# A scan's exponentials moved into the block of short products, in a one-core hybrid encoder layer

## The chip, the core and the metric

The kernel runs on one core of one Trainium2 chip. The metric is the device time of one execution in microseconds, the median of the runs shown. The engines are named as in the profile: PE (matrix products; PEld is its weight load), DVE, ACT, POOL, and SP, which here only issues DMAs.

## What is computed

One layer of a streaming encoder for 256 frames of a new stream and 8 x 16 frames of running streams, 384 tokens in all, model width 2048. Float32 accuracy is kept by splitting each operand into a high and a low part and taking three products.

```python
proj = u @ p['w_in']                      # pool | z | x, B, C | dt | gates
xbc, new_conv = causal_conv(xbc, st_conv, p['conv_w'], p['conv_b'])
...
def step(h, inp):                         # the scan, per chunk
    cum = jnp.cumsum(dtc * A, axis=1)
    seg = cum[:, :, None] - cum[:, None, :]
    decay = jnp.exp(jnp.where(causal, seg, -jnp.inf))
    cb = jnp.einsum('btgn,bsgn->btsg', Cc, Bc)
    y = jnp.einsum('btsgr,bsgrp->btgrp', cb[..., None] * decay, xdt)
    y = y + jnp.einsum('btgn,bgrpn->btgrp', Cc, h) * jnp.exp(cum)[..., None]
    h = h * jnp.exp(last)[..., None, None] + jnp.einsum('bsgn,bsgr,bsgrp->bgrpn', Bc, w_end, xdt)
...
h = y * silu(z)                           # gated RMSNorm, one norm per group
m = sigmoid(g_A) * (A @ w_pool_proj) + sigmoid(g_B) * (B @ w_ssd_proj);  x += RMSNorm(m @ w_out)
x += RMSNorm(relu(RMSNorm(x) @ w_up)^2 @ w_down)
```

The scan has 8 groups of 8 heads. The change lies in this scan, which takes the stretch from 478 to 1300 us of the span.

## The kernel before

The scan phase walks over the 8 groups. Per group there are ten projections of 128 channels by 384 tokens: B, C, x0 to x3 and z0 to z3. Each is two *units* (`proj_units`), one for each half of the 2048 input channels: a weight tile of 128 x 1024 is loaded, split (`wh` by a copy on ACT, `wl` by a subtraction on DVE; `wturn`), and multiplied by 24 matmuls (`half`, L188 to L190). `flow` sets the order on all engines, as the code is recorded in one order and each engine works through its part in that order. For unit i it issues the load of unit i + 4 on SP, the products of unit i on PE, the split of unit i + 3 (`prep`), then the unit's eviction `post`, and then `work`, which takes tasks from the queue `todo` until their costs have used up the budget of a unit. `need` empties that queue up to a named task. The pools hold three tiles of weights, three of each split part (every fourth pair has buffers of its own, L143 and L144), and PSUM has two banks for projections (`banks(mm=2, ss=6)`), so that a projection has to wait until the one before the last is evicted.

A *block* (`block(old, new)`) is a run of short products on PE: `Y` of the older half group (masked decay times values, L677), `yi` of the newer one (state times C, L697), the older one's new prompt state `pp`, and transposes of the newer one's x (and of B, with `cb`, at a first half). DVE then evicts: `yis`, the older x with its skip, `xdt` and `xdw` (x by dt and by the decay to the end), `cbm`. Each group has two blocks: that of its first half stands behind x2's second unit, that of its second half behind z3's.

After a block, tasks go into `todo`:

- `state_tasks`: the part of `xdw` for the running streams is split (`xhl`: ACT, then DVE, L797 and L798) and written by SP to `x_scr`. `xst_load` reads it back in another layout (L907), behind eight loads `bst_load` (L898) at a first half. `update` multiplies it by B (`su`, L920, PE) and adds it to the state `hs` (L924, DVE). The update of a first half stands between the two units of z1, that of a second half between the two units of the next group's x0.
- `decay_state`: the state is multiplied by its decay (L782).
- `decay_tasks`: per pair of heads a tile `E` of exponentials from `cbc` (cumulative sums, broadcast by a load on SP): 8 short calls and two longer ones on ACT.
- `gated_tasks`: `zs` times `xs` on DVE, the square (`ssum`, `ysq`) on ACT.
- `decay_masks`: `E` times `cbm` on DVE (L861).

ACT holds one table of functions at a time; the order has an ACT_TABLE_LOAD wherever exponentials follow `silu` or the reverse.

Of the kernel before, what the change touches and what calls it, by code (L numbers as in the profile page):

```python
# [7 lines left out]
F32 = mybir.dt.float32  # L8
F32R = mybir.dt.float32r
I32 = mybir.dt.int32  # L10
AF = mybir.ActivationFunctionType
ALU = mybir.AluOpType
# [3 lines left out]
P = 128  # L16
T = 384
TP = 256
NB = 8
# [3 lines left out]
G = 8  # L23
# [39 lines left out]
def build(ctx, tc, io):  # L63
    nc = tc.nc
    v, s, te, gp, sy = nc.vector, nc.scalar, nc.tensor, nc.gpsimd, nc.sync
# [48 lines left out]
    def later(cost, tag, f):  # L114
        todo.append((cost, tag, f))
# [9 lines left out]
    def need(*tags):  # L125
        while any(t in tags for _, t, _ in todo):
            cost, _, f = todo.popleft()
            f()
            debt[0] -= cost
# [123 lines left out]
    x_scr = [dram.tile([P, 2, 2, P], F32, name=f"x_scr{i}") for i in range(16)]  # L253
# [117 lines left out]
    decb = small.tile([P, NH, NB], F32, name="decb")  # L371
    with tc.tile_pool(name="phc", bufs=1, reuse_waits="tile") as pc, tc.tile_pool(name="phc2", bufs=2, reuse_waits="tile") as pc2:
        bufs = []
        for i in range(2):
            b = pc.tile([P, 519], F32, name=f"pbuf{i}")
# [173 lines left out]
    nothing = lambda *_: None  # L549
    phd = ExitStack()  # L550
    pd = phd.enter_context(tc.tile_pool(name="phd", bufs=2, reuse_waits="tile"))
# [8 lines left out]
    for i in range(2):  # L560
        b = pd1.tile([P, 24, 19], F32, name=f"cbuf{i}")
# [87 lines left out]
        sy.dma_start(hs, io["ssm"][g * 2 + hf])  # L649

    def cbc_load(g, hf):
        need(f"exp{g}_1" if hf else f"exp{g - 1}_3")
        for j in (hf * 2, hf * 2 + 1):
            cbc = S[g]["cbc"][j] = pd.tile([P, 2, T], F32, tag="cbc", name=f"cbc{g}_{j}")
            sy.dma_start(cbc, cum_scr[g * 8 + j * 2 : g * 8 + j * 2 + 2, :].partition_broadcast(P))
# [10 lines left out]
    def block(old, new):  # L666
        Y = []
        if old:
            g, hf = old
            need(f"E{g}_{hf * 2}", f"E{g}_{hf * 2 + 1}")  # L670
            d = S[g]
# [13 lines left out]
        if new:  # L685
            g2, h2 = new
# [5 lines left out]
            hs = d2["hs"][h2]  # L692
# [70 lines left out]
                cbm = d2["cbm"] = pd.tile([P, 512], F32, tag="cbm", name=f"cbm{g2}", bufs=1)  # L763
                v.tensor_tensor(cbm, cb, cst2[:, :512], ALU.mult)
        if new:
            state_tasks(g2, h2)
            decay_state(g2, h2)
            decay_tasks(g2, h2)
            final = new == (G - 1, 1)
            if final:  # L770
                decay_masks(g2, h2)
        if old:
            gated_tasks(g, hf)
        if new and not final:
            decay_masks(g2, h2)

    def decay_state(g, hf):
        hs, h0 = S[g]["hs"][hf], g * 8 + hf * 4

        def decay():  # L780
            hv = hs.rearrange("p b (h q) -> p b h q", h=4)
            v.tensor_tensor(  # L782
                hv,
                hv,
                decb[:, h0 : h0 + 4, :].rearrange("p h b -> p b h").unsqueeze(3).to_broadcast([P, NB, 4, 64]),
                ALU.mult,
            )

        later(2.3, f"dec{g}_{hf}", decay)

    def state_tasks(g, hf):
        d = S[g]

        def parts():
            xhl = pd.tile([P, 2, 2, P], F32R, tag="xhl", name=f"xhl{g}_{hf}", bufs=1)
            x = d["xdw"][hf][:, :, 2, :]
            s.activation(xhl[:, 0], x, AF.Copy)  # L797
            v.tensor_tensor(xhl[:, 1], x, xhl[:, 0].bitcast(F32), ALU.subtract)  # L798
            sy.dma_start(x_scr[g * 2 + hf], xhl.bitcast(F32))

        later(0.5, f"xhl{g}_{hf}", parts)

    def gated_tasks(g, hf):
        d = S[g]

        def gated(j):
            z = d["zs"][j]
            v.tensor_tensor(z, z, d["xs"][j], ALU.mult)
            if j == 0:
                d["ssum"] = pd.tile([P, T], F32, tag="ssum", name=f"ssum{g}", bufs=1)  # L810
                s.activation(d["ssum"], z, AF.Square)
            else:
                d["q"] = pd.tile([P, T], F32, tag="ysq", name=f"ysq{g}_{j}", bufs=1)
                s.activation(d["q"], z, AF.Square)

        def add():
            v.tensor_tensor(d["ssum"], d["ssum"], d["q"], ALU.add)

        def parts():
            add()  # L820
            d["sh"] = pd.tile([P, T], F32R, tag="sh", name=f"sh{g}", bufs=1)
            d["sl"] = pd.tile([P, T], F32R, tag="sl", name=f"sl{g}", bufs=1)
            s.activation(d["sh"], d["ssum"], AF.Copy)
            v.tensor_tensor(d["sl"], d["ssum"], d["sh"].bitcast(F32), ALU.subtract)

        j = hf * 2
        later(0.6, f"gt{g}_{j}", lambda: (add() if j else None, gated(j)))
        later(0.6 if hf else 1.2, f"gt{g}_{j + 1}", lambda: (add() if j else None, gated(j + 1)))
        if hf:
            later(1.1, f"sum{g}", parts)  # L830

    def decay_tasks(g, hf):
        d = S[g]
        for j in (hf * 2, hf * 2 + 1):
            h0 = g * 8 + j * 2

            def head(hh, j=j, h0=h0):
                if hh == 0:
                    d["E"][j] = pd.tile([P, 2, 512], F32, tag="E", name=f"E{g}_{j}")
                E, cbc, h = d["E"][j], d["cbc"][j], h0 + hh  # L840
                s.activation(E[:, hh, P:TP], cbc[:, hh, P:TP], AF.Exp, bias=tok[:, 9, h : h + 1])
                for b, e0 in enumerate((0, TP, T)):
                    s.activation(
                        E[:, hh, e0 : e0 + P], cbc[:, hh, b * P : b * P + P], AF.Relu, bias=tok[:, b, h : h + 1], scale=-1.0
                    )

            def powers(j=j):
                E = d["E"][j]
                s.activation(E[:, :, :P], E[:, :, :P], AF.Exp, scale=-1.0)
                s.activation(E[:, :, TP:], E[:, :, TP:], AF.Exp, scale=-1.0)  # L850

            later(0.6, None, lambda head=head: head(0))
            later(0.8, f"exp{g}_{j}", lambda head=head, powers=powers: (head(1), powers()))

    def decay_masks(g, hf):
        d = S[g]
        for j in (hf * 2, hf * 2 + 1):

            def masked(j=j):
                E = d["E"][j]  # L860
                v.tensor_tensor(E, E, d["cbm"].unsqueeze(1).to_broadcast([P, 2, 512]), ALU.mult)  # L861

            later(1.3, f"E{g}_{j}", masked)
# [46 lines left out]
            )  # L910

    def update(g, hf):
        need(f"dec{g}_{hf}")
        hs, xst, bs = S[g]["hs"][hf], S[g]["xst"], bst
        su = []
        for r in range(4):
            o = sstile(f"su{g}_{hf}_{r}")
            su.append(o)
            for b in range(2):
                te.matmul(o[:, b * 256 : b * 256 + 256], bs[:, r, b, :], xst[:, r, :], start=True, stop=True)  # L920

        def add(r):
            hr = hs[:, r * 2 : r * 2 + 2, :].rearrange("p b n -> p (b n)")
            v.tensor_tensor(hr, hr, su[r], ALU.add)  # L924
            if r == 3:
                gp.dma_start(io["new_ssm_s"][g * 2 + hf], hs)

        for r in range(3, -1, -1):
            todo.appendleft((0.7, f"su{g}_{hf}" if r == 3 else None, lambda r=r: add(r)))
# [12 lines left out]
    for g in range(G):  # L942
        u0 = 17 + g * 10
        xu = lambda j: conv_units(u0 + 2 + j, g * 4 + j, "xs", 6, put(g, "xs", j))
        items += conv_units(u0, 32 + g, "BT", 1, put(g, "BT"))
        if g:
            at(xst_load, g - 1, 1)
        items += conv_units(u0 + 1, 40 + g, "CT", 1, put(g, "CT"), lambda g=g: make_Cm(g))
        u = xu(0)
        items += u[:1]  # L950
        if g:
            at(update, g - 1, 1)
        items += u[1:]
        at(cbc_load, g, 0)
        items += xu(1)
        u = xu(2)
        items += u[:1]
        items.append((*u[1][:3], nothing))
        at(block, (g - 1, 1) if g else None, (g, 0))
        at(u[1][3])  # L960
        u = xu(3)
        items += u[:1]
        at(lambda g=g: (need(f"su{g - 1}_1"), hs_load(g, 1)))
        items += u[1:]
        at(bst_load, g)
        at(xst_load, g, 0)
        items += z_units(g, 0)
        u = z_units(g, 1)
        items += u[:1]
        at(update, g, 0)  # L970
        items += u[1:]
        u = z_units(g, 2)
        items += u[:1]
        if g:
            at(norm_mm, g - 1)
        items += u[1:]
        u = z_units(g, 3)
        items += u[:1]
        at(cbc_load, g, 1)
        items += u[1:]  # L980
        at(block, (g, 0), (g, 1))
        if g < G - 1:
            at(lambda g=g: (need(f"su{g}_0"), hs_load(g + 1, 0)))

# [35 lines left out]
    at(update, G - 1, 1)  # L1020
    items += tail_[4:5]
    at(block, (G - 1, 1), None)
    at(narrow)
    items += tail_[5:8]
    at(norm_mm, G - 1)
# [201 lines left out]

    hs_load(0, 0)
    wide[0] = pd1
    begin, rest = flow(items, budget=3.2)  # L1230
    begin()
    xs2, pga_hold = [], ExitStack()

# [617 lines left out]
```

## Time and profile before

| what | us |
|---|---|
| median of 3 runs | 2798.18 (2797.39 to 2800.08) |
| profiled execution, its time | 2798.07 |
| its span | 2796.3 |
| PE busy | 2762.0 |
| DVE busy | 1825.3 |
| ACT busy | 1346.2 |
| scan phase (478 to 1300 us): PE, DVE, ACT busy | 799.15, 581.52, 453.08 of 822.0 |

A row of the timeline gives start and duration in us, the engine, the line of the kernel, the operation with the tile written and those read (buffer numbers left out), the shapes, how often it runs in a row, and in brackets how long the engine stood idle before it and what released it. A row of the waits gives the total in us, the times, and the longest. "SPq" is SP's queue of DMA issues. A DMA's start there is its issue, not its landing.

### The profile page before, as it was taken

The numbers are of one execution on the slowest core, as the hardware profiler recorded it, in microseconds if no ns is written. First come the engines' busy times: TensorE is split into PE (matmuls) and PEld (weight loads), VectorE is DVE, ScalarE is ACT, GpSimd is POOL, SyncE is SP. The second block draws the span as 40 slices with busy tenths as digits, with TensorE's granted clock in tenths as the row PEclk, the third lists the DMA queues.
The fourth block names the chain that finished last, engine by engine and source line by source line (L and its number), as shares of the span: only waits on it lengthen the run. The fifth ranks groups of instructions, "written<-read, shape, count | busy, mean of one in ns | idle before, by whom it ended". The sixth has DMA issues, their size and how long they took to land.

```text
span 2796.3 us, 38572 instructions
## 1 busy us (share of the span) xinstructions
PE 2762.0 (99%) x14961; PEld 2517.0 (90%) x14961; DVE 1825.3 (65%) x2421; ACT 1346.2 (48%) x2181; POOL 222.1 (8%) x334
## 2 busy tenths in 40 slices
PE   9999999999999999999999999999999999999998
PEld 9998888999999999998888888899999999998987
DVE  8755333667777767767533333648887788778878
ACT  6433323556556465564522223535555555555663
POOL 0000000000000000001000000000011111111221
PEclk9999999999999999999999999999999999999999
DMA  6444444456556555545844454444566868777787
GB/s 223 135 131 144 145 145 166 164 175 211 185 187 205 203 177 197 203 162 192 285 150 150 151 196 136 147 155 181 183 172 167 203 174 216 182 192 181 174 242 243
DMA packets 166328, 505.37 MB, mean 181 GB/s; under 512 B 20544, under 2 KB 39808, under 8 KB 161280
## 3 DMA queue, kind: packets, MB, share of 16 engines
q1 hardware_dynamic: 132000, 409.22, 42.9%
q0 software_dynamic: 34000, 93.68, 14.2%
q8 instruction: 117, 1.92, 0.3%
q14 instruction: 67, 0.55, 0.1%
q10 hardware_dynamic: 144, 0.01, 0.0%
HBM read 413.93 MB, written 88.90 MB: 180 GB/s over the span
## 4 chain that ended last, share of the span: by engine, by line
PE 80%; DVE 10%; ACT 5%; issue 2%; DMA 1%; SPq 0%; POOL 0%; DVEq 0%; ACTq 0%
PE pj_up L188 6%; PE pj_up L189 6%; PE pj_up L190 6%; PE wd L1507 5%; PE wd L1508 5%; PE wd L1506 5%; PE pj_sp L207 3%; PE pj_sp L209 3%; PE pj_sp L208 3%; PE pj_x L188 3%; PE pj_x L189 3%; PE pj_x L190 3%; PE pj_gb L207 2%; PE wo L208 2%; PE pj_ga L208 2%
## 5 line engine op out<-in xcount | busy, mean ns | idle before, releaser
L1360 ACT ACTIVATE wh_wd<-raw 128x1024 fp32r<-128x1024 f32 x210 | 222.8, 1061 | 255.3 <-PE pj_up L189 103.9
L188 PE MATMUL pj_up<-x1h,wh_up 128*128 128x384 f32 x992 | 334.1, 337 | 0.0
L189 PE MATMUL pj_up<-x1l,wh_up 128*128 128x384 f32 x992 | 333.3, 336 | 0.0
L190 PE MATMUL pj_up<-x1h,wl_up 128*128 128x384 f32 x992 | 333.3, 336 | 0.0
L1361 DVE TENSOR_TENSOR wl_wd<-raw,wh_wd 128x1024 fp32r<-128x1024 f32 x210 | 256.8, 1223 | 97.2 <-ACT wh_wd L1360 96.4
L188 PE MATMUL pj_x<-xgh,wh_x 128*128 128x384 f32 x768 | 257.8, 336 | 0.0
L190 PE MATMUL pj_x<-xgh,wl_x 128*128 128x384 f32 x768 | 256.7, 334 | 0.0
L189 PE MATMUL pj_x<-xgl,wh_x 128*128 128x384 f32 x768 | 256.6, 334 | 0.0
L1507 PE MATMUL wd<-wl_wd,fh 128*128 128x512 f32 x588 | 229.1, 390 | 0.2 <-DVE wl_wd L1361 0.2
L1506 PE MATMUL wd<-wh_wd,fh 128*128 128x512 f32 x588 | 229.0, 389 | 0.0
L1508 PE MATMUL wd<-wh_wd,fl 128*128 128x512 f32 x588 | 228.8, 389 | 0.0
L1360 ACT ACTIVATE wh_up<-w_up 128x1024 fp32r<-128x1024 f32 x123 | 130.2, 1059 | 127.7 <-issue 66.5
L188 PEld LDWEIGHTS pj_up<-x1h,wh_up 128*128 128x128 f32 x992 | 186.5, 188 | 4.0
L189 PEld LDWEIGHTS pj_up<-x1l,wh_up 128*128 128x128 f32 x992 | 186.5, 188 | 4.0
L190 PEld LDWEIGHTS pj_up<-x1h,wl_up 128*128 128x128 f32 x992 | 186.5, 188 | 0.0
L1361 DVE TENSOR_TENSOR wl_up<-w_up,wh_up 128x1024 fp32r<-128x1024 f32 x123 | 150.2, 1222 | 55.3 <-ACT wh_up L1360 55.3
L188 PE MATMUL pj_z<-xgh,wh_z 128*128 128x384 f32 x512 | 172.3, 337 | 11.0 <-DVE zs L641 11.0
L190 PE MATMUL pj_z<-xgh,wl_z 128*128 128x384 f32 x512 | 172.7, 337 | 9.0 <-DVE wl_z L104 9.0
L104 DVE TENSOR_TENSOR wl_sp<-w_sp,wh_sp 128x1024 fp32r<-128x1024 f32 x64 | 78.1, 1225 | 153.0 <-ACT wh_sp L103 152.6
L189 PE MATMUL pj_z<-xgl,wh_z 128*128 128x384 f32 x512 | 171.8, 336 | 0.0
L1522 POOL DMA_DIRECT2D acc_scr<-ev x144 | 122.9, 902 | 572.3 <-ACT ev L1518 567.5
L103 ACT ACTIVATE wh_sp<-w_sp 128x1024 fp32r<-128x1024 f32 x64 | 67.8, 1062 | 173.0 <-PE pj_sp L209 168.5
(373 smaller groups left out, 6626.1 us busy)
## 6 DMA issues: line engine op xcount, KB each, us to landing
w_up<-w_up SPq DMA_DIRECT2D x126, 512.0 KB, 5.2
raw<-w_down SPq DMA_DIRECT2D x112, 512.0 KB, 5.9
w_x<-w_in SPq DMA_DIRECT2D x96, 512.0 KB, 4.3
acc_scr<-ev POOLq DMA_DIRECT2D x168, 256.0 KB, 5.7
w_z<-w_in SPq DMA_DIRECT2D x64, 512.0 KB, 4.4
w_sp<-w_ssd SPq DMA_DIRECT2D x64, 512.0 KB, 3.3
w_ga<-w_gate SPq DMA_DIRECT2D x32, 512.0 KB, 3.3
w_pp<-w_pp SPq DMA_DIRECT2D x32, 512.0 KB, 3.2
```

What stands on the lines that cost most here:

```text
L188: te.matmul(out, wh, xh, start=first, stop=False)
L189: te.matmul(out, wh, xl, start=False, stop=False)
L190: return te.matmul(out, wl, xh, start=False, stop=last)
L207: te.matmul(o, ah, wh[:, c], start=k == 0, stop=False)
L208: te.matmul(o, ah, wl[:, c], start=False, stop=False)
L209: te.matmul(o, al, wh[:, c], start=False, stop=k == 2 * n - 1)
L1360: s.activation(h, w, AF.Copy)
L1361: return (h, l), lambda: v.tensor_tensor(l, w, h.bitcast(F32), ALU.subtract)
L1506: te.matmul(o, ah, wh[:, cols], start=c_first[c] == r and k2 == 0, stop=False)
L1507: te.matmul(o, ah, wl[:, cols], start=False, stop=False)
L1508: te.matmul(o, al, wh[:, cols], start=False, stop=c_last[c] == r and k2 == 1)
L1522: gp.dma_start(acc_scr[p][c], e, accum_op=ALU.add)
```

## The change

Five edits, all in the scan phase:

1. `decay_tasks` and the ACT part of `state_tasks` become `exponentials`, which the block calls at its end: both tiles of `E` are computed without a break, the copy of `xhl` between them. The low part of `xhl` and the write of `x_scr` stay a task.
2. The new function `behind` runs after the block and after the eviction of the projection: the state decay and the first of a half's two gated products are done there at once, no longer as tasks.
3. z3's eviction is moved behind the block of the second half, as x2's was at the first.
4. `cbc_load` and `update` no longer empty the queue up to the exponentials and the decay.
5. The scan's budget of a unit falls from 3.2 to 2.6.

```diff
     def cbc_load(g, hf):
-        need(f"exp{g}_1" if hf else f"exp{g - 1}_3")
...
         if new:
-            state_tasks(g2, h2)
-            decay_state(g2, h2)
-            decay_tasks(g2, h2)
-            final = new == (G - 1, 1)
-            if final:
-                decay_masks(g2, h2)
+            exponentials(g2, h2)
+
+    def behind(old, new):
+        if new:
+            decay_state(*new)
         if old:
-            gated_tasks(g, hf)
-        if new and not final:
-            decay_masks(g2, h2)
+            gated_tasks(*old)
+        if new:
+            decay_masks(*new)
...
     def gated_tasks(g, hf):
...
-        later(0.6, f"gt{g}_{j}", lambda: (add() if j else None, gated(j)))
+        if j:
+            add()
+        gated(j)
         later(0.6 if hf else 1.2, f"gt{g}_{j + 1}", lambda: (add() if j else None, gated(j + 1)))
...
-    def decay_tasks(g, hf):
+    def exponentials(g, hf):
         d = S[g]
+        x = d["xdw"][hf][:, :, 2, :]
         for j in (hf * 2, hf * 2 + 1):
             h0 = g * 8 + j * 2
...
+            E = d["E"][j] = pd.tile([P, 2, 512], F32, tag="E", name=f"E{g}_{j}")
+            cbc = d["cbc"][j]
+            for hh in range(2):
+                h = h0 + hh
                 s.activation(E[:, hh, P:TP], cbc[:, hh, P:TP], AF.Exp, bias=tok[:, 9, h : h + 1])
...
+            s.activation(E[:, :, :P], E[:, :, :P], AF.Exp, scale=-1.0)
+            s.activation(E[:, :, TP:], E[:, :, TP:], AF.Exp, scale=-1.0)
+            if j % 2 == 0:
+                xhl = pd.tile([P, 2, 2, P], F32R, tag="xhl", name=f"xhl{g}_{hf}", bufs=1)
+                s.activation(xhl[:, 0], x, AF.Copy)
+
+        def low():
+            v.tensor_tensor(xhl[:, 1], x, xhl[:, 0].bitcast(F32), ALU.subtract)
+            sy.dma_start(x_scr[g * 2 + hf], xhl.bitcast(F32))
+
+        later(0.5, f"xhl{g}_{hf}", low)
...
     def update(g, hf):
-        need(f"dec{g}_{hf}")
...
         at(cbc_load, g, 1)
-        items += u[1:]
+        items.append((*u[1][:3], nothing))
         at(block, (g, 0), (g, 1))
+        at(u[1][3])
+        at(behind, (g, 0), (g, 1))
...
-    begin, rest = flow(items, budget=3.2)
+    begin, rest = flow(items)
```

How this moves instructions is shown for group 1; the other groups are alike. In the names, `E1_0` is the tile of the group's first pair of heads, `wh_z1_0_1` the high part of the weights of z0's second unit (`z1_0` is z0 of group 1), `x6` is x2 of group 1, `x42` its successor's C.

On ACT, behind the block of group 1's first half, before the change:

```order
L760 ACTIVATE Bhl1_5400<-trB1_5375 128x128
L586 COPY cbuf0_3981<-cstate_3979 128x8x3
L588 COPY cbuf0_3981<-cbuf0_3981 128x15x3
L591 ACTIVATE cacc6_5409<-cbuf0_3981,vec_70 128x384
L592 COPY cstate_3979<-cbuf0_3981 128x27
L103 ACTIVATE wh_z1_0_1_5439<-w_z1_0_1_5299 128x1024
L600 ACTIVATE xs6_5446<-cacc6_5409,vec_70 128x384
L797 ACTIVATE xhl1_0_5448<-xdw1_0_5391 128x256
```

On ACT at the same place after it, the start and (behind the six other rows of `E1_1`) the end of the piece:

```order
L759 ACTIVATE Bhl1_5400<-trB1_5375 128x128
L825 ACT_TABLE_LOAD
L825 ACTIVATE E1_0_5406<-cbc1_0_5189,tok_689 128x128
L827 ACTIVATE E1_0_5406<-cbc1_0_5189,tok_689 128x128 x3
L825 ACTIVATE E1_0_5406<-cbc1_0_5189,tok_689 128x128
L827 ACTIVATE E1_0_5406<-cbc1_0_5189,tok_689 128x128 x3
L830 ACTIVATE E1_0_5406<-E1_0_5406 128x2x128
L831 ACTIVATE E1_0_5406<-E1_0_5406 128x2x256
L834 ACTIVATE xhl1_0_5417<-xdw1_0_5391 128x256
L825 ACTIVATE E1_1_5419<-cbc1_1_5191,tok_689 128x128
```

And its end:

```order
L831 ACTIVATE E1_1_5419<-E1_1_5419 128x2x256
L586 COPY cbuf0_3981<-cstate_3979 128x8x3
L588 COPY cbuf0_3981<-cbuf0_3981 128x15x3
L591 ACTIVATE cacc6_5433<-cbuf0_3981,vec_70 128x384
L592 COPY cstate_3979<-cbuf0_3981 128x27
L796 ACTIVATE ysq0_2_5439<-zs0_2_4783 128x384
L103 ACTIVATE wh_z1_0_1_5468<-w_z1_0_1_5299 128x1024
L600 ACT_TABLE_LOAD
```

A table load, two tiles of exponentials and a square now stand ahead of the conv's copy and of `wh_z1_0_1`; before, they followed seven to ten rows later.

On DVE, at the same block, behind the eviction of x2 (`cbuf0`), before the change:

```order
L587 TENSOR_TENSOR cbuf0_3981<-pj_x6_5270,rstd_159 128x24x16
L104 TENSOR_TENSOR wl_z1_0_1_5440<-w_z1_0_1_5299,wh_z1_0_1_5439 128x1024
L596 SCALAR_TENSOR_TENSOR cacc6_5409<-cbuf0_3981,vec_70,cacc6_5409 128x384 x3
L798 TENSOR_TENSOR xhl1_0_5448<-xdw1_0_5391,xhl1_0_5448 128x256
L782 TENSOR_TENSOR hs1_0_4915<-hs1_0_4915,decb_690 128x2048
L104 TENSOR_TENSOR wl_z1_1_0_5482<-w_z1_1_0_5412,wh_z1_1_0_5481 128x1024
```

On DVE after it:

```order
L587 TENSOR_TENSOR cbuf0_3981<-pj_x6_5270,rstd_159 128x24x16
L778 TENSOR_TENSOR hs1_0_4943<-hs1_0_4943,decb_690 128x2048
L799 TENSOR_TENSOR ssum0_4941<-ssum0_4941,ysq0_1_4979 128x384
L790 TENSOR_TENSOR zs0_2_4783<-zs0_2_4783,xs2_4515 128x384
L104 TENSOR_TENSOR wl_z1_0_1_5469<-w_z1_0_1_5299,wh_z1_0_1_5468 128x1024
L596 SCALAR_TENSOR_TENSOR cacc6_5433<-cbuf0_3981,vec_70,cacc6_5433 128x384 x3
L837 TENSOR_TENSOR xhl1_0_5417<-xdw1_0_5391,xhl1_0_5417 128x256
```

The decay and the gated product moved ahead of the split; the low part of `xhl`, which SP's write of `x_scr` waits for, still stands behind that split and the conv taps. SP's rows stand in the same order before and after.

On ACT, behind the block of group 1's second half, after the change (the row ahead of it is the second tile of exponentials; before, `wh_x42_1` stood directly behind the block's copy `pe`, ahead of the first exponential):

```order
L831 ACTIVATE E1_3_5919<-E1_3_5919 128x2x256
L642 ACT_TABLE_LOAD
L642 ACTIVATE zs1_3_5930<-zs1_3_5930 128x384
L793 ACTIVATE ssum1_5935<-zs1_0_5607 128x384
L143 ACTIVATE wh_x42_1_5966<-w_x42_1_5809 128x1024
```

There the weights of the next group's C wait for both tiles, a table load, z3's `silu` and a square.

More of the change, by code (lines that the diff above doesn't have):

```diff
@@ L765, in block @@
         if new:
-            state_tasks(g2, h2)
-            decay_state(g2, h2)
-            decay_tasks(g2, h2)
-            final = new == (G - 1, 1)
-            if final:
-                decay_masks(g2, h2)
+            exponentials(g2, h2)
+    def behind(old, new):
+        if new:
+            decay_state(*new)
         if old:
-            gated_tasks(g, hf)
-        if new and not final:
-            decay_masks(g2, h2)
+            gated_tasks(*old)
+        if new:
+            decay_masks(*new)
     def decay_state(g, hf):
         hs, h0 = S[g]["hs"][hf], g * 8 + hf * 4
[L780 to L801, printed above, removed]
+        hv = hs.rearrange("p b (h q) -> p b h q", h=4)
+        v.tensor_tensor(
+            hv,
+            hv,
+            decb[:, h0 : h0 + 4, :].rearrange("p h b -> p b h").unsqueeze(3).to_broadcast([P, NB, 4, 64]),
+            ALU.mult,
+        )
     def gated_tasks(g, hf):
@@ L830, in gated_tasks @@
             later(1.1, f"sum{g}", parts)
-    def decay_tasks(g, hf):
+    def exponentials(g, hf):
         d = S[g]
+        x = d["xdw"][hf][:, :, 2, :]
         for j in (hf * 2, hf * 2 + 1):
             h0 = g * 8 + j * 2
[L837 to L840, printed above, removed]
+            E = d["E"][j] = pd.tile([P, 2, 512], F32, tag="E", name=f"E{g}_{j}")
+            cbc = d["cbc"][j]
+            for hh in range(2):
+                h = h0 + hh
                 s.activation(E[:, hh, P:TP], cbc[:, hh, P:TP], AF.Exp, bias=tok[:, 9, h : h + 1])
@@ L845, in head @@
                     )
[L847 to L853, printed above, removed]
+            s.activation(E[:, :, :P], E[:, :, :P], AF.Exp, scale=-1.0)
[7 more added lines that the diff above has]
+        later(0.5, f"xhl{g}_{hf}", low)
     def decay_masks(g, hf):
@@ L960, in build @@
         at(u[1][3])
+        at(behind, (g - 1, 1) if g else None, (g, 0))
         u = xu(3)
@@ L1022, in build @@
     at(block, (G - 1, 1), None)
+    at(behind, (G - 1, 1), None)
     at(narrow)
```

## The prediction

> **What bounds the kernel now.** I read the page's busy times first, then the list of waits on PE, then one group of the scan instruction by instruction: PE, then ACT, DVE and SP's DMA queue around the same block. From the page:
>
> ```profile
> PE 2762.0 (99%) x14961; PEld 2517.0 (90%) x14961; DVE 1825.3 (65%) x2421; ACT 1346.2 (48%) x2181; POOL 222.1 (8%) x334
> ```
>
> PE is busy 99% of the span, so less work on ACT or DVE is worth nothing by itself. The change can only take away or add time in which PE stands still. The list of waits on PE (us in total, times, longest) has three rows over 1.2 us that lie in the scan:
>
> ```profile
> PE pj_z L188 <- DVE zs L641: 11.0, 8, 1.8
> PE pj_z L190 <- DVE wl_z L104: 9.0, 6, 1.5
> PE su L920 <- DMA xst<-x_scr: 1.5, 2, 0.9
> ```
>
> The first two are the prize: 20.0 us, about 2.5 in each of eight groups. The third is short, but it tells that the state update `su` starts as soon as its transfer has landed, in two groups out of eight even later than PE would like. PE around group 1's first half (start, duration):
>
> ```profile
> 592.58 1.11 PE L920 MATMUL su<-xst,bst 128*128 128x256 f32 x8
> 614.43 1.96 PE L677 MATMUL Y<-E,xdt 128*64 128x256 f32 x24
> ...
> 641.77 1.19 PE L920 MATMUL su<-xst,bst 128*128 128x256 f32 x8
> 648.50 0.41 PE L188 MATMUL pj_z<-xgh,wh_z 128*128 128x384 f32 x1 [1.37 <-DVE zs L641]
> ```
>
> Five half products lie between 593.5 (`su` 592.58 and its 0.95 us of issue) and 614.43, so a half product is 4.18 us: the pace at which split weights must arrive. ACT in the same stretch:
>
> ```profile
> 620.26 0.28 ACT L760 ACTIVATE Bhl<-trB 128x128 fp32r<-128x128 f32 x1
> ...
> 622.74 0.24 ACT L588 COPY cbuf<-cbuf 128x45 f32<-128x45 f32 x1 [2.10 <-DVE cbuf L587]
> ...
> 623.64 1.06 ACT L103 ACTIVATE wh_z<-w_z 128x1024 fp32r<-128x1024 f32 x1
> ...
> 628.36 0.40 ACT L797 ACTIVATE xhl<-xdw 128x256 fp32r<-128x256 f32 x1
> ...
> 636.57 1.28 ACT L841 ACT_TABLE_LOAD   x1
> ...
> 642.00 0.39 ACT L841 ACTIVATE E<-cbc,tok 128x128 f32<-128x128 f32 x1
> ...
> 645.17 0.51 ACT L814 ACTIVATE ysq<-zs 128x384 f32<-128x384 f32 x1
> 645.59 1.04 ACT L103 ACTIVATE wh_z<-w_z 128x1024 fp32r<-128x1024 f32 x1
> ```
>
> One tile of exponentials takes 3.17 us (642.00 to 645.17). The pair runs from 636.57 to 645.17, and the weights of z2 come behind it at 645.59: that is why PE stands at 648.50. DVE:
>
> ```profile
> 624.74 1.23 DVE L104 TENSOR_TENSOR wl_z<-w_z,wh_z 128x1024 fp32r<-128x1024 f32 x1 [2.03 <-ACT wh_z L103]
> 625.88 1.92 DVE L596 SCALAR_TENSOR_TENSOR cacc<-cbuf,vec,cacc 128x384 f32<-128x384 f32 x3
> 628.79 0.43 DVE L798 TENSOR_TENSOR xhl<-xdw,xhl 128x256 fp32r<-128x256 f32 x1 [0.99 <-ACT xhl L797]
> ...
> 651.57 2.35 DVE L861 TENSOR_TENSOR E<-E,cbm 128x1024 f32<-128x1024 f32 x2
> 653.84 2.35 DVE L104 TENSOR_TENSOR wl_z<-w_z,wh_z 128x1024 fp32r<-128x1024 f32 x2
> ```
>
> The second stall of a group (`pj_z L190`) waits for the split at 653.84, which the two masks at 651.57 hold up. And SP's queue, group 1 and the last group:
>
> ```profile
> 629.25 0.33 SPq L799 DMA_DIRECT2D x_scr<-xhl  x1
> ...
> 630.64 6.71 SPq L898 DMA_DIRECT2D bst<-b_scr  x8
> 637.40 1.85 SPq L907 DMA_DIRECT2D xst<-x_scr  x4
> 639.29 2.42 SPq L96 DMA_DIRECT2D w_z<-w_in  x3
> ```
>
> ```profile
> 1241.76 1.85 SPq L907 DMA_DIRECT2D xst<-x_scr  x4
> 1246.32 1.11 PE L920 MATMUL su<-xst,bst 128*128 128x256 f32 x8
> ```
>
> This is the row to remember. SP works in order: the write of `xhl` at 629.25, then a state load, a weight load, eight loads of `bst`, four of `xst`, the last issued by 639.25. `su` begins 2.5 us later, at 641.77. From the issue of that write to `su` it is 12.5 us with nothing to spare.
>
> **The change, part by part.** *Exponentials into the block.* In the first half of a group ACT now does, straight behind `Bhl` (free at 620.43): table load 1.28, two tiles 6.34 with the `xhl` copy 0.40 between them, the four small conv steps 1.0 (622.74 to 623.64, and 0.1), the square `ysq` 0.42, and only then the `wh_z` of z0's second half: it starts at 629.87 instead of 623.64 and ends at 630.93. PE needs it at 633.2 (three half products behind the block's end at 620.6), its low part at 633.5: DVE delivers that by 632.1. No stall there.
>
> *The low part of xhl.* Behind that split DVE does three conv taps (1.92), then `xhl` (0.43): 630.97 + 1.14 + 1.92 + 0.43 = 634.46, against 629.22 before. SP's write of `x_scr` leaves at 634.4 instead of 629.25, 5.1 us later (4.7 in group 0, which has no older block and so no `ysq`). Everything that SP has behind it moves along: state load, weight load, `bst`, `xst`. So `su` moves from 641.77 to about 646.9. On PE's path only the `su` of the first half counts: 7 x 5.1 + 4.7 = 40.4. Groups with some slack take less: the last group's `su` starts 2.71 behind its last issue, 0.2 more than group 1's 2.52. I take 0.15 a group, 1.2 in all: **+39 us**. Bounds: 0 if SP's stretch shrinks by as much (rival 1), 45 if each `su` moves by 5.6.
>
> *State decay and first gated product directly behind.* DVE does the 2.29 us decay, a sum and a product while it would wait for ACT anyway (from 622.65 to 630.9). Cost nothing; cover gone, 3.2 us, but ACT's 6 us are longer.
>
> *Eviction behind.* x2's was behind its block already. z3's product is evicted behind the four `xdw`, a few us later, and its PSUM bank is wanted two half products behind the block: hidden. x3's eviction follows the split of z1's first half, which is itself behind `xhl` and the next square, at about 638.3 by the same durations; PE's z1 begins about 1 us late; but PE then stands at `su` until 646.9 anyway, so this is inside the 39.
>
> *The stalls that go.* The exponentials are done by 628.5 and the masks run while PE waits at `su`; both stalls behind them go: **-20.0 us**. What is late next is the weight fetch of z2: it stands behind `xst` in SP's queue. Rows of SP's weight loads in the window from 639 to 641, us from issue to landing:
>
> ```profile
> DMA to landing us min/median/max: 4.6/4.9/5.3
> ```
>
> Issue + 4.9 + 1.04 (`wh`) + 1.14 (`wl`) + 0.55 (z0's eviction, which frees the bank) is 7.7 behind the last `xst`; PE comes there 2.5 + 0.95 + 4.18 = 7.6 behind it. I put 0.2 a group: **+2 us** (bounds 0 and 4).
>
> *The second half* has the same pile-up with more room. Rows of block (1,1) and the tail:
>
> ```profile
> 667.45 1.96 PE L677 MATMUL Y<-E,xdt 128*64 128x256 f32 x24
> 672.64 0.35 ACT L741 COPY pe<-pp 128x256 f32<-128x256 f32 x1
> 693.29 1.11 PE L920 MATMUL su<-xst,bst 128*128 128x256 f32 x8
> ...
> 1272.37 1.96 PE L677 MATMUL Y<-E,xdt 128*64 128x256 f32 x24
> ...
> 1295.12 1.12 PE L920 MATMUL su<-xst,bst 128*128 128x256 f32 x8
> ```
>
> ACT from at latest 672.9: load 1.28, tiles and copy 6.74, load back 1.28, `silu` and square 0.95, `wh` 1.06: 684.2; `wl` by 685.4. `pe` waited there for z3's eviction, which now comes later, so it can start some 0.6 earlier: 683.6 and 684.8. PE wants these at 684.9 and 685.3. `x_scr` then leaves at 685.2 to 685.9 (before: 677.4), and 2.2 + 2.5 + 2.5 later `su` could start: 693.1 at worst, needed at 693.29. So nothing is paid, barely. In the tail the units are shorter: the chain wants about 24.1 behind `Y` (17.7 + 2.2 + 1.8 + 2.5), PE is there after 22.75: **+1.3**.
>
> *Tables.* 13 of 52 loads go, 13 x 1.28 = 16.7 us of ACT, off PE's path; the one load that moves ahead of `wh_z` is in the sum above with 1.28. The Trainium skill ("ScalarE: Activation LUTs", What ACT_TABLE_LOAD costs) puts a switch at 2.66 us with its drain; by that the sum would be some 11 us worse. The trace disagrees: the load at 636.57 is followed by work in 1.3 us, so the row decides.
>
> *Sum*: 39 - 20.0 + 2 + 1.3 = +22.3 us. The profiled execution took 2798.07 us, within 0.1 of the median 2798.18; predicted 2820 us, 0.8% slower.
>
> **The rivals.** *1, faster: SP's stretch shrinks.* The eight `bst` issues take 6.71 us, and part of that is waiting for transfers:
>
> ```profile
> SPq L898 <- DMA w_z<-w_in: 10.1, 8, 1.4
> SPq L898 <- DMA hs<-ssm: 9.8, 8, 1.5
> ```
>
> That is 2.5 us a group. If that wait, and a similar part of the slow issues, were for loads already in flight before `x_scr`, they would be over by 634.4, and `su` would move by about 1.6 only: 8 x 1.6 - 20 + 1 = -6, **2792**. The sign turns at a shift of about 2.4 a group; at that point nothing is measured (2798). Against it: the state load and the weight load stand behind `x_scr` in the queue, so they move along.
>
> *2, the clock.* PE would stand about 4 us at each `su`, longer than anywhere now. A cold start is at the head of the trace, the first two products of one size:
>
> ```profile
> 4.70 0.65 PE L320 MATMUL pj_p<-xgh,wh_o 128*128 128x384 f32 x1
> 5.19 0.34 PE L321 MATMUL pj_p<-xgh,wl_o 128*128 128x384 f32 x1
> ```
>
> The cold one takes twice as long. If the clock fell at each wait and PE ran one half product at half speed before it is back, that costs up to 8 x 1.7 = 14: **2834**. The longest idle on PE in the scan now is under 2 us, and no drop is seen behind it. The Trainium skill ("TensorE: Matmul & The Clock Gate", Why this matters for your kernels) says to avoid gaps over about 3 us for this reason; no run here has shown such a gap yet.
>
> *3, the second half misses.* If its split comes 1 to 1.5 us late in seven groups, +9: **2829**. For it: a margin of 0.1 to 0.5 us, worked out over eight instructions.
>
> **How the numbers follow.** A difference under 0.2% (5.6 us) can't be told from none here. The forecast, 2820, has 0.60, with 2810 to 2829 as its own range; rival 1 0.07 for faster and 0.06 for a shift that just cancels; the clock 0.11; the second half 0.16. Slower is 0.60 + 0.11 + 0.16 = 0.87. The range runs from 2804, which leaves out the cases without a loss, to 2836, which takes in the clock's whole price.
>
> **What would show it.** In the changed kernel: `x_scr<-xhl` leaves some 14 us behind the block of a first half instead of 8.7; PE's list of waits has `su <- xst` with 30 to 40 us over eight waits of 3 to 5 us each, and the rows `pj_z <- zs` and `pj_z <- wl_z` shrink to a few us. The prediction is wrong if `su` starts as early as now behind its block, if PE waits at `pj_x` behind second halves, or if the granted clock dips at `su`.

## The result and the profile after

The changed kernel took 2838.3 us (median of four runs, 2835.4 to 2842.0), the kernel before 2798.6 (2797.4 to 2800.1) on the same chip: a ratio of 1.0142, interval 1.0125 to 1.0160. So it is 39.7 us slower, where 22 were predicted and 2836 was the upper end. The profiled execution took 2841.95 us (span 2840.2), the slowest of the four; against the span before, 2796.3, that is 43.9.

The page's busy times and the list of waits on PE, changed kernel (us in total, times, longest):

```profile
PE 2780.7 (98%) x14961; PEld 2530.3 (89%) x14961; DVE 1828.0 (64%) x2421; ACT 1333.5 (47%) x2168; POOL 221.5 (8%) x334
```

```profile
PE su L906 <- DMA xst<-x_scr: 30.5, 8, 5.7
PE pj_z L188 <- DVE cbuf L587: 9.6, 7, 1.4
PE su L906 <- DMA w_z<-w_in: 4.3, 1, 4.3
PE pj_x L190 <- DVE wl_x L144: 3.0, 5, 0.6
```

The two stalls that were to go (`pj_z <- zs`, `pj_z <- wl_z`, 20.0 us) are gone, and `su` waits 34.8 us in nine waits, one in each first half and one at the scan's end (the tail). But look at the first line too: PE has the same 14961 instructions and is busy 18.7 us longer (2762.0 before). The products themselves became slower, and the prediction's sum has no term for that. The granted clock of PE (1.00 is full speed) shows it: it falls to 0.50 nine times between 548 and 1340 us, for 37.5 us in all. Before, it falls once in the scan, for 3.4 us.

Group 1's first half on PE, ACT, DVE and SP's queue (start, duration; in brackets the idle time before):

```profile
621.97 1.96 PE L676 MATMUL Y<-E,xdt 128*64 128x256 f32 x24
623.85 1.12 PE L696 MATMUL yi<-hs,Cm 128*32 128x128 f32 x32
...
646.42 0.41 PE L188 MATMUL pj_z<-xgh,wh_z 128*128 128x384 f32 x1 [1.37 <-DVE cbuf L587]
653.80 2.04 PE L906 MATMUL su<-xst,bst 128*128 128x256 f32 x8 [2.95 <-DMA xst<-x_scr]
655.64 0.52 PE L188 MATMUL pj_z<-xgh,wh_z 128*128 128x384 f32 x1
655.97 0.52 PE L189 MATMUL pj_z<-xgl,wh_z 128*128 128x384 f32 x1
```

```profile
628.13 1.28 ACT L825 ACT_TABLE_LOAD   x1
...
635.61 0.62 ACT L831 ACTIVATE E<-E 128x512 f32<-128x512 f32 x1
...
637.14 0.52 ACT L796 ACTIVATE ysq<-zs 128x384 f32<-128x384 f32 x1
637.57 1.04 ACT L103 ACTIVATE wh_z<-w_z 128x1024 fp32r<-128x1024 f32 x1
```

```profile
638.64 1.23 DVE L104 TENSOR_TENSOR wl_z<-w_z,wh_z 128x1024 fp32r<-128x1024 f32 x1 [4.70 <-ACT wh_z L103]
639.78 1.92 DVE L596 SCALAR_TENSOR_TENSOR cacc<-cbuf,vec,cacc 128x384 f32<-128x384 f32 x3
641.62 0.42 DVE L837 TENSOR_TENSOR xhl<-xdw,xhl 128x256 fp32r<-128x256 f32 x1
```

```profile
642.11 0.33 SPq L838 DMA_DIRECT2D x_scr<-xhl  x1
642.54 0.37 SPq L649 DMA_DIRECT2D hs<-ssm  x1
642.96 0.44 SPq L96 DMA_DIRECT2D w_z<-w_in  x1
643.50 5.57 SPq L885 DMA_DIRECT2D bst<-b_scr  x8
649.11 1.85 SPq L894 DMA_DIRECT2D xst<-x_scr  x4
```

The chain is the one foretold: exponentials, square, `wh_z`, `wl_z`, taps, low part, `x_scr`, `xst`, `su`. The write leaves 18.3 us behind `yi`; before, with the write at 629.25, it was 12.9 behind this row:

```profile
616.32 1.12 PE L697 MATMUL yi<-hs,Cm 128*32 128x128 f32 x32
```

Behind the wait `su` takes 2.04 us instead of 1.19, and the half product's matmuls follow each other every 0.31 to 0.32 us instead of 0.17 until 657.2; the granted clock is 0.50 from 653.8 to 657.2 and 1.00 on both sides.

The scan cut at the starts of `yi` and `su`, summed from the timelines of profiled executions (us; the two right columns belong to experiments 2 and 11 below):

| stretch | before | changed | useless products at the wait | masks direct |
|---|---|---|---|---|
| `yi` of a first half to its `su`, 8 | 202.5 | 244.0 | 237.7 | 202.5 |
| that `su` to the next block's `yi`, 8 | 218.2 | 207.4 | 193.2 | 201.7 |
| second halves, `yi` to `yi`, 7 | 333.8 | 341.7 | 337.6 | 334.7 |

### The profile page after: what moved, and what is told of

The parts are those of the page before. It is cut to its first block, busy times and chain, and to the rows that moved or that the text cites. A ratio compares the mean times of both kernels' runs of the same rounds, so it can differ in the third digit from the quotient of the medians.

```text
span 2840.2 us, 38567 instructions
## 1 busy us (share of the span) xinstructions
PE 2780.7 (98%) x14961; PEld 2530.3 (89%) x14961; DVE 1828.0 (64%) x2421; ACT 1333.5 (47%) x2168; POOL 221.5 (8%) x334
## 4 chain that ended last, share of the span: by engine, by line
PE 82%; ACT 7%; DMA 5%; DVE 4%; issue 1%; SPq 1%; DVEq 0%; POOL 0%; ACTq 0%
PE pj_up L188 6%; PE pj_up L189 6%; PE pj_up L190 6%; PE wd L1497 5%; PE wd L1498 5%; PE wd L1496 5%; PE pj_sp L207 3%; PE pj_sp L208 3%; PE pj_sp L209 3%; PE pj_x L190 2%; PE pj_x L188 2%; PE pj_x L189 2%; PE pj_z L188 2%; PE pj_z L189 2%; PE pj_z L190 2%; DMA w_z<-w_in 2%
## 5 line engine op out<-in xcount | busy, mean ns | idle before, releaser
L188 PE MATMUL pj_up<-x1h,wh_up 128*128 128x384 f32 x992 | 334.1, 337 | 0.0
L190 PE MATMUL pj_up<-x1h,wl_up 128*128 128x384 f32 x992 | 333.3, 336 | 0.0
L190 PE MATMUL pj_x<-xgh,wl_x 128*128 128x384 f32 x768 | 257.9, 336 | 3.0 <-DVE wl_x L144 3.0
L188 PE MATMUL pj_x<-xgh,wh_x 128*128 128x384 f32 x768 | 258.9, 337 | 0.0
L188 PEld LDWEIGHTS pj_up<-x1h,wh_up 128*128 128x128 f32 x992 | 186.5, 188 | 4.0
L190 PEld LDWEIGHTS pj_up<-x1h,wl_up 128*128 128x128 f32 x992 | 186.5, 188 | 0.0
L188 PE MATMUL pj_z<-xgh,wh_z 128*128 128x384 f32 x512 | 175.9, 343 | 9.6 <-DVE cbuf L587 9.6
L190 PE MATMUL pj_z<-xgh,wl_z 128*128 128x384 f32 x512 | 174.3, 340 | 0.0
```

Of the source, the lines that this page charges most:

```text
L188: te.matmul(out, wh, xh, start=first, stop=False)
L190: return te.matmul(out, wl, xh, start=False, stop=last)
```

## The experiments

Times are medians, ratios are to the kernel before on the same chip (2797.2 to 2797.4 us in all jobs), with 95% intervals. The 2838.3 us of the changed kernel stand beside 2798.6 for the kernel before, so differences from it are uncertain by about 1 us.

**1. The low part written at once.** The task that held it is called right behind the first gated product:

```diff
             gated_tasks(*old)
         if new:
+            S[new[0]]["low"]()
             decay_masks(*new)
...
-        later(0.5, f"xhl{g}_{hf}", low)
+        d["low"] = low
```

> The changed kernel with one task moved: the low part of xhl and the write of x_scr are done straight behind the block's first gated product instead of waiting in the task queue behind the split of wh_z and three conv taps. Theory A (the write of x_scr leaves too late, PE stands idle at su, and its clock drops there): the write leaves about 12.5 us behind Y instead of 20.1; the transfer that su needs has then landed about 24.2 us behind Y, and PE comes to su after 27.5, so the 34.8 us of waits at su go, and the slow products behind them (about 15 us) go too; the bank wait of z1 (9.6) stays or shrinks by 0.4 a group. Time about 2786 (2780 to 2794), faster than the kernel before. Rival B (the 8 us of exponentials on ACT themselves hold PE back, through late weights or late evictions, and su's wait only hides that): new waits of 3 us and more a group at pj_z or pj_x take the place, 2815 to 2838.

2796.8 us, ratio 0.9998 (0.9989 to 1.0008): as fast as before, 41.5 less than the changed kernel. Half of the expectation came, and the time lies 3 us above its range; rival B's waits of 3 us and more did not come. No wait at `su` is left; the write leaves 9.8 us behind `yi`. But the bank stall at z1 grew:

```profile
PE pj_z L188 <- DVE cbuf L587: 14.9, 7, 2.1
```

The low part had cost the queue 0.5 of its budget; without it the sum of squares, with two round trips between DVE and ACT, came in ahead of z1's split and x3's eviction. Behind four of the seven stalls of 2.1 us PE ran at half speed, as behind `su` in the changed kernel.

**2. Useless products at the wait.**

```diff
         hs, xst, bs = S[g]["hs"][hf], S[g]["xst"], bst
+        if hf == 0:
+            idle = sstile(f"idle{g}")
+            for _ in range(16):
+                te.matmul(idle[:, :T], xg[0][0][:, :P], xg[0][0], start=True, stop=True)
```

> The changed kernel with 16 useless products of 384 columns (2.8 us at full speed) on PE ahead of each first half's su, while PE would wait for xst. The writes leave as late as before. Theory A (idle time lowers the clock): su still cannot start earlier, but it runs in 1.1 us instead of 2.0 and the next half product starts at full speed: 2838 - 15 = 2823 (2818 to 2828). Rival C (the slow products are not due to the idle time, but to something at that place, such as the transfers or the reads of weights): su and the products behind it stay slow, 2838 to 2842.

2817.0 us, ratio 1.0070 (1.0055 to 1.0085): 21.3 us come back though PE does more work; that is 1 us below the expected range. `su` runs in 1.1 to 1.2 us, and in the first halves no half product behind it is slow: the granted clock falls once, in the tail, where no useless products stand. Theory A holds, rival C falls. From the table: 14.2 us (207.4 to 193.2) lie behind `su`, which is the clock; 6.3 lie ahead of it: `su` starts 0.8 us earlier behind `yi` on average, and why its transfers land sooner stays open.

**3. The state update one half product later.** `update(g, 0)` stands behind z1's second unit instead of between its two.

> The changed kernel with the first half's su one half product (4.18 us) later on PE, between z1 and z2 instead of inside z1. The write of x_scr leaves as late as in the changed kernel. Theory A: waits of 2.9 to 4.4 us plus the 1.37 of the bank fall to 0 to 1 a group, the clock stays up: about 2792 (2785 to 2800). Rival B (exponentials themselves are the limit: weights and evictions behind them): the wait goes from su to pj_z, 2815 to 2838.

2814.5 us, ratio 1.0061 (1.0046 to 1.0076): 24 us better, 14 above theory A's range and at the edge of rival B's. The wait at `su` goes in all eight first halves (the tail keeps its 3.9), but others take a good part of its place:

```profile
PE pj_z L188 <- DVE cbuf L587: 9.2, 7, 1.3
PE pj_z L188 <- DVE zs L641: 9.1, 8, 3.0
PE pj_z L190 <- DVE wl_z L144: 5.1, 8, 0.6
PE su L906 <- DMA xst<-x_scr: 4.1, 2, 3.9
```

So moving the reader is worth less than moving the write: DVE's order around z1 and z2 is late as well.

**4, 5 and 7. Which part makes the write late.** In number 4, exponentials, copy, low part and write are tasks again, the rest as changed:

```diff
-            exponentials(g2, h2)
+            state_tasks(g2, h2)
+            decay_tasks(g2, h2)
```

> The changed kernel with one part undone: the exponentials, the copy of xhl, its low part and the write of x_scr are tasks of the queue again as in the kernel before. State decay and first gated product stay directly behind the block, the evictions stay behind, the queue's budget stays 2.6. Theory A (all of the loss comes from the exponentials' place, through x_scr): about 2798 (2790 to 2804), with the two stalls at pj_z back or partly back. Rival D (decay and gated product on DVE, or the late evictions, cost PE time by themselves): 2810 or more.

In number 7 the first gated product is a task again too:

```diff
-        gated(j)
-        later(..., lambda: (..., gated(j + 1)))
+        for j in (hf * 2, hf * 2 + 1):
+            later(..., lambda j=j: (..., gated(j)))
```

> The fourth experiment's kernel (exponentials as tasks) with the first gated product a task again; the state decay stays directly behind the block on DVE, evictions behind, budget 2.6. Theory A2: without the square on ACT ahead of it, wh of z0's second half starts at once, and its low part waits only for the decay's end, about 1 us: the write of x_scr leaves about 16 us behind Y instead of 18.3, su waits about 1 us, too short for the clock: 2800 to 2812. Rival G (evictions behind, or the smaller budget, are what costs): 2825 or more, no change from 2836.8.

In number 5, on the kernel before, the exponentials alone move into the block:

```diff
-            state_tasks(g2, h2)
+            exponentials(g2, h2)
             decay_state(g2, h2)
-            decay_tasks(g2, h2)
```

> The kernel before with one part of the change alone: the exponentials and the copy of xhl are issued as part of the block, the low part stays a task; decay, gated products, evictions and the budget of 3.2 are as in the kernel before. Theory A2 (two things each hold up the split of z0's second half on their own, the 8 us of exponentials on ACT, or the square of the first gated product, which waits for decay and product on DVE; together they cost hardly more than one): the write of x_scr leaves about 19.5 us behind Y (14.8 before, 20.1 changed), su waits 3.5 to 4.5 us in each group, the clock drops, the two stalls at pj_z go: 2825 to 2838. Rival E (the parts add up, so that what undoing the exponentials saved, 1.6 us, is all they cost): 2796 to 2804.

Measured: number 4, 2836.8 us (1.0140; 1.0125 to 1.0155); number 7, 2812.9 (1.0057; 1.0042 to 1.0072); number 5, 2827.5 (1.0110; 1.0093 to 1.0127). Number 4 was a plain miss: with the exponentials undone hardly anything came back. Its trace shows why:

```profile
628.25 0.55 DVE L802 TENSOR_TENSOR ssum<-ssum,ysq 128x384 f32<-128x384 f32 x1
628.72 0.55 DVE L793 TENSOR_TENSOR zs<-zs,xs 128x384 f32<-128x384 f32 x1
630.81 1.23 DVE L104 TENSOR_TENSOR wl_z<-w_z,wh_z 128x1024 fp32r<-128x1024 f32 x1 [1.54 <-ACT wh_z L103]
```

```profile
629.30 0.53 ACT L799 ACTIVATE ysq<-zs 128x384 f32<-128x384 f32 x1 [2.13 <-DVE zs L793]
629.73 1.04 ACT L103 ACTIVATE wh_z<-w_z 128x1024 fp32r<-128x1024 f32 x1
```

ACT is free, but `wh_z` stands behind the square, and the square waits for the product, which DVE does behind the decay. So the first gated product holds up the same split that the exponentials hold up. The write leaves 16.4 us behind `yi` there, 13.85 in number 7, 17.8 in number 5, 18.25 in the changed kernel, 12.9 to 13.1 before. For the write the parts do not add up: each hides behind the other.

The totals are less plain. Cut as in the table above, the first halves (its first two rows together) are 440.2 us long in number 4 and 441.2 in number 5, 420.7 before and 451.4 in the changed kernel: with the exponentials undone 11.2 us do come back there. But the second halves of number 4 take 352.9 us, 11.2 more than in the changed kernel; in group 1 both tiles of exponentials run there in one piece, from 684.50 to 692.16 with the table load, ahead of the next `wh_x`. That number 4 is as slow as the changed kernel is therefore in part chance. Number 5 came inside its range as theory A2, formed on number 4, had it: 30.2 us of waits at `su`, and both stalls at `pj_z` gone. Number 7 came within 1 us of its range, but by another road: not with 1 us a group at `su`, but with stalls of 2.7 us at `pj_z L188` in seven groups, four of them with a fall of the clock. Rival E falls, and for number 7 rival G.

**8, 9 and 12. Evictions and the queue's budget.** Number 8 is number 7 with the state decay a task again, number 9 that with the budget of 3.2. Number 12 is the kernel before with z3's eviction alone put behind its block:

```diff
-        items += u[1:]
+        items.append((*u[1][:3], nothing))
         at(block, (g, 0), (g, 1))
+        at(u[1][3])
```

Number 8:

> The seventh experiment's kernel with the state decay a task again as well: against the kernel before only the evictions of both blocks' projections behind and the budget of 2.6 remain. Theory A2: neither costs anything, 2798 (2794 to 2804). Rival G: 2810 or more.

Number 9:

> The eighth experiment's kernel with the queue's budget back at 3.2: against the kernel before only the evictions of both blocks' projections behind remain. Theory H (with all work still in the queue, a budget of 2.6 a unit lets it pile up, until a need pulls it in at one place; that made 2852): 2795 to 2806. Rival G (the late evictions do it): 2835 or more.

Number 12:

> The kernel before with one move alone: z3's product is evicted behind the second half's block instead of ahead of it; the tasks of the queue keep their order (in the eighth and ninth experiments the state decay had also come to stand behind the exponentials in the queue), the budget stays 3.2. Theory I (the late eviction itself is hidden, and those two kernels lost their 54 us to the order of the queue, where a need for the decay pulls both tiles of exponentials in ahead of the splits of z1): 2798 (2793 to 2806), the waits at pj_z and su as in the kernel before. Rival G (the late eviction costs by itself, through the table load for silu that comes after it): 2820 or more, with waits at pj_x in the second half.

Number 8 took 2851.9 us (1.0195; 1.0180 to 1.0210), number 9 2851.7 (1.0194; 1.0179 to 1.0209), number 12 2805.2 (1.0028; 1.0017 to 1.0038). Theory A2 missed number 8 by 48 us at its upper end, and theory H fell with number 9. The two take the same time, but they lose it in different places: the first halves take 431.6 us in number 8 and 456.4 in number 9, the second halves 373.6 and 347.4. The budget moves the loss, and that the sums are equal is chance. z3's eviction alone costs 7.9 (number 12, inside theory I's range), so the other 46 are left to what else those kernels change, the order of the queue (the decay stands behind the exponentials in it), alone or together with the eviction; it was not tried by itself. The traces fit it: in group 1 of number 9 the second tile of exponentials ends directly ahead of the `wh_z` at 648.77, for which PE waits 2.87 us, and in number 8 both tiles (684.28 to 691.93, with the table load) stand directly ahead of a `wh_x`. The list of waits on PE in number 12:

```profile
PE pj_z L188 <- DVE zs L641: 12.2, 7, 2.1
PE pj_z L190 <- DVE wl_z L104: 6.0, 4, 1.5
PE pj_x L190 <- DVE wl_x L144: 5.0, 6, 0.9
```

The third row is new against the kernel before, and the second halves are 6.8 us longer there (340.6 against 333.8). So the late eviction is not quite hidden in the kernel before. In number 11 below, which has it too, the second halves are only 0.9 longer: what it costs hangs on the work around it.

**10. The budget in the changed kernel.** `flow(items, budget=3.2)`.

> The changed kernel with the budget back at 3.2. Theory A2 (in the changed kernel the write of x_scr, ordered behind split and taps, sets su, whatever the budget): the same waits of 3 to 5.7 us at su and the same slow products: 2838 (2832 to 2844). Rival H' (the smaller budget is a good part of the loss here too): 2820 or less.

2822.1 us, ratio 1.0087 (1.0072 to 1.0102). Theory A2 missed by 10, rival H' by 2: the budget is a good part of the loss here.

```profile
PE pj_z L188 <- DVE cbuf L587: 17.3, 7, 2.5
PE su L906 <- DMA xst<-x_scr: 17.1, 7, 4.0
```

The write leaves as late as in the changed kernel (18.2 behind `yi`), but the wait is cut in two: up to 2.5 us at z1's bank, and the rest at `su`. The first halves are 17.1 us shorter (434.3 against 451.4). Of the eight waits at `su` in the scan's first halves one is still 4.0 us and none of the others reaches 2.9, and PE is busy 8.6 us less (2772.1): the granted clock falls five times instead of nine. Two short waits keep it more often than one long one.

**6. Sum and masks queued later.** Experiment 1, with the second gated product, the sum and the masks queued behind x3's eviction (all three through `defer`):

```diff
-        later(..., f"gt{g}_{j + 1}", ...)
+        defer(..., f"gt{g}_{j + 1}", ...)
...
         items += u[1:]
+        at(release)
         at(bst_load, g)
```

> The kernel with the low part written straight behind the block (first experiment) and one more move: the second gated product, the sum of squares and the masks of that block are queued only behind the eviction of x3, so that nothing but the conv taps stands between the split of z0's second half and that of z1's first. Theory A2: the remaining stall (2.13 us in seven groups at z1's bank, and the four clock drops behind it, 1.6 us each) goes: wh of z1 starts 2 us earlier. 2797 - 14.9 - 6.5 = 2775 (2772 to 2784). Rival F (PE's pace is so tight that the deferred work delays the next split as much): a stall of about 2 us a group shows one unit later, at pj_z L188 or L190, 2790 to 2800.

2800.3 us, ratio 1.0011 (1.0002 to 1.0020): rival F, at the upper edge of its range. The stall is as long and one unit later, at z0's eviction, which now stands behind sum and mask:

```profile
PE pj_z L188 <- DVE zs L641: 13.7, 7, 2.0
```

**11. Masks direct.** Instead of waiting in the queue, the second gated product and both masks go where DVE stands idle, behind the block:

```diff
-        gated(j)
-        later(..., lambda: (..., gated(j + 1)))
+        product(j)
+        square(j)
+        product(j + 1)
+        defer(0.6, ..., lambda: (add() if j else None, square(j + 1)))
...
-            later(1.3, f"E{g}_{j}", masked)
+            masked()
```

> The sixth experiment's kernel, and in the 5 us in which DVE stands idle behind the block it now also does the second gated product and both masks (0.55 and 2.35 us); only the squares' sums stay in the queue, behind the eviction of x3. Theory A2: no DVE work with a wait on ACT stands between the splits of z0, z1 and z2 any more: the seven stalls of 1.96 us (13.7) and five clock drops (8) go: 2800 - 21 = 2779 (2773 to 2785), faster than the kernel before. Rival F (the deferred work delays the next split wherever it is put): a stall of about 2 us a group shows at a third place, 2792 to 2802.

2780.5 us, ratio 0.9939 (0.9922 to 0.9955): 17 us faster than the kernel before and 58 faster than the changed one, the best of all. Its DVE around group 1's block, its write on SP's queue, and PE's waits:

```profile
623.75 1.02 DVE L802 TENSOR_TENSOR zs<-zs,xs 128x384 f32<-128x384 f32 x2
624.69 0.42 DVE L854 TENSOR_TENSOR xhl<-xdw,xhl 128x256 fp32r<-128x256 f32 x1
625.02 1.22 DVE L865 TENSOR_TENSOR E<-E,cbm 128x1024 f32<-128x1024 f32 x1
627.30 1.23 DVE L865 TENSOR_TENSOR E<-E,cbm 128x1024 f32<-128x1024 f32 x1 [1.05 <-ACT E L848]
629.68 1.23 DVE L104 TENSOR_TENSOR wl_z<-w_z,wh_z 128x1024 fp32r<-128x1024 f32 x1 [1.16 <-ACT wh_z L103]
```

```profile
625.14 0.33 SPq L855 DMA_DIRECT2D x_scr<-xhl  x1
```

```profile
PE pj_z L188 <- DVE zs L641: 6.0, 7, 0.9
PE pj_x L188 <- DVE cbuf L587: 0.4, 1, 0.4
```

The write is on its way 10.2 us behind `yi`, the low part and the masks are done in the gap that DVE spends on ACT anyway, and no wait is longer than 0.9 us, and in this scan the granted clock does not fall at all. Rival F falls for this place; the 0.85 that is left per group is the sum of squares ahead of z0's eviction.

## Why the prediction was right or wrong

*The shift of `su`: right.* Put at 39; the stretch from `yi` to `su` grew by 41.5 (202.5 to 244.0), of which 9.6 are z1's bank stall, counted as inside it. The write itself moved by 5.2 to 5.3 us in groups 1 to 7, forecast 5.1. But the trace alone gave the cause too simply. The decay and the first gated product, costed at nothing because ACT's exponentials are longer, were hidden by them and would have held the same split without them: the write is 2.6 us later with the product direct than with it as a task (16.4 and 13.85 behind `yi`, experiments 4 and 7).

*The stalls that go: right in kind.* Both rows are gone. With the clock held up (experiment 2), the stretch behind `su` shrinks by 25.0, more than the forecast 20.0 less 2 for z2's weights; no wait for those is seen.

*The clock: the step that failed.* It was set aside as a rival at 0.11, with the sentence that the longest idle now is under 2 us and no drop is seen behind it. That sentence was wrong by the trace of before itself. PE there, group 7's first half:

```profile
1253.42 0.41 PE L188 MATMUL pj_z<-xgh,wh_z 128*128 128x384 f32 x1 [1.83 <-DVE zs L641]
1253.67 0.34 PE L189 MATMUL pj_z<-xgl,wh_z 128*128 128x384 f32 x1
...
1254.45 0.52 PE L190 MATMUL pj_z<-xgh,wl_z 128*128 128x384 f32 x1
1254.77 0.52 PE L188 MATMUL pj_z<-xgh,wh_z 128*128 128x384 f32 x1
1255.09 0.52 PE L189 MATMUL pj_z<-xgl,wh_z 128*128 128x384 f32 x1
```

Behind 1.83 us of idling the matmuls come every 0.32 us from 1254.45 on, until 1257.7; the granted clock is 0.50 from 1254.3 to 1257.7. Read right, these rows would have said that waits of 3 to 5 us, which the forecast itself placed on PE eight times, were likely to drop the clock. It was never an alternative to the forecast but a consequence of it, and its price belonged in the sum. Measured: about 14 us in the first halves, the figure that stood in the rival.

*The second half: the other step that failed.* Forecast at no cost "barely"; the seven stretches are 7.9 us longer, near the 9 of rival 3, though by another road. The split of C's second unit came in time (`wh` ended 14.4 us behind `yi` in group 1, forecast 14.3 to 14.9); the waits are at later units, `pj_x L190`, 0.6 each. The list counts 3.0 of the 7.9 as waits; the clock does not fall in these stretches, and the rest is spread over single products of `pj_x` that follow each other later than every 0.17 us. "Hidden" for z3's eviction was a wrong term: alone it makes these stretches 6.8 longer (experiment 12). How much of the 7.9 it causes in the changed kernel is not shown, since in number 11 it costs hardly anything.

*The tail* was put at 1.3; from the last `yi` to the end it is 5.1 longer (1527.1 against 1522.0). The wait at its `su` is 3.6, and its products were slow behind it as well. *The budget* of 2.6 instead of 3.2 was not costed at all, and is worth 16 us here (experiment 10).

*Rival 1* did not come: `x_scr` to the last `xst` issue stayed at 8.9 to 10.4 us, 9.1 to 10.7 before.

So three things that were each put at none or left to a rival (clock 14, second halves 8, tail 4 more than forecast) make 26 us, the stalls gave about 7 more than forecast, and the shift took 2.5 more; together some 21 of the 21.6 between the forecast's 22.3 and the profiled execution's 43.9.

## What to carry to other kernels

Where a forecast puts a wait of some microseconds on TensorE, add to each the slow products behind it, and look in the old trace for the longest idle spots and the spacing of the products right behind them. Two pieces of work that delay the same instruction do not add up, and each can look free because the other covers it: ask of every cover what is under it. Two kernels of equal time can lose it in different places (numbers 8 and 9): cut the span into stretches before saying that a part makes no difference. When work has to leave a queue, look for the gap where its engine waits anyway; put one slot later (experiment 6) it only moved the stall.

## What the runs showed of the hardware

In the scan of all fourteen traces I took every idle spot of PE of 0.5 us and more and the granted clock behind it. Of the waits of 2.9 us and more, 21 of 22 went with half speed; of those between 1.7 and 2.9 us, 35 of 57 (of the seven equal stalls of 2.1 us in experiment 1, four); below 1.6 us none that stood alone.

The middle band looks like chance and is not. Within one execution the granted clock changes only at points of a fixed grid with steps of 3.413 us: in the changed kernel it falls at 548.0, 653.8, 759.6, 865.4, 971.2, 1077.0 and 1182.9, each time 31 steps apart, and it stays at 0.50 for one step or two (3.4 or 6.8 us). In the scan and its tail the thirteen traces with such falls have 62 of them (number 11 has none). Ahead of every one PE stood idle for 1.83 us or more of the step that had just ended, by the profile's count, and every step with more than 1.89 us of idling ended in a fall. So a wait of 2 us drops the clock when it lies within one step and not when it straddles two, and short waits can do it together: in numbers 8 and 9 five falls stand behind waits that were each under 1.6 us. Where PE is busy, one step at half speed costs half its length, 1.7 us. The Trainium skill ("TensorE: Matmul & The Clock Gate", What's actually happening) describes a free-running window of about 3.4 us that decides on the clock; the grid agrees with that. The advice of the same page (Why this matters for your kernels) to avoid gaps of over about 3 us is too generous for this kernel: 1.83 us were enough where they fell into one step.
